# Four product pairs of seven in the down projection of a decoder layer, and the order of the first gate/up pairs

## The chip, the cores and the metric

The kernel runs on one core of a Trainium2 chip. The metric is the device time of one execution in microseconds (us). Before the change three runs took 1966.54, 1968.5 and 1970.39 us: the median is 1968.5.

The engines are called as in the profile: PE is TensorE (PEld its weight load), DVE is VectorE, ACT is ScalarE, POOL is GpSimd, and SP issues the DMAs.

## What is computed

One layer of a decoder with attention, short convolution, a SwiGLU block and a gated embedding, in fp32, for 1024 prompt tokens and 64 sample tokens. The change is in the SwiGLU block:

```
h = rmsnorm(x, norm_ffn)
gu = h @ w_gate_up                      # 1024 x 5632
g, u = gu[..., :D_FF], gu[..., D_FF:]   # D_FF = 2816 = 22 x 128
x = x + (jax.nn.silu(g) * u) @ w_down   # 2816 x 1024
gate = jax.nn.sigmoid(rmsnorm(x, norm_ple) @ w_ple_gate)
return x + (p @ w_ple) * gate
```

## The kernel before

Activations stand transposed, features on the 128 partitions and the 1088 tokens as columns. The second half of the kernel cuts the tokens into two problems, p = 0 and p = 1, of 544 columns, and each into two halves of CW = 272. Every fp32 operand is split into a high and a low part, and a product is three matmuls: high by high, high by low, low by high (`mmg`, L155).

**Gate/up** (`run_pair`, L2372) multiplies by seven products instead of eight. One pair takes column block f of the gate and of the up half, eight row blocks of h as two times four, and one problem p: a 2 by 2 by 2 block product in seven products (`ORDER` 1, 6, 7, 5, 2, 4, 3), each four row blocks x three matmuls = 12 matmuls of 272 columns, 84 in all. Three sides of it cost vector work:

- The activations of a problem need seven factors for each of four row blocks (`factors`, L1819): four half-width tensor operations, the high parts on ACT, and the low parts on DVE, three of 544 columns and one of 272. In the names, `f0` and `f1` are the factors of p = 0 and p = 1. For gate/up they are made out of `norm` (L1930), which writes the normed rows with four operations (L140) per block.
- The weights of a pair arrive as four raw blocks (`wraw`, 256 KB each) and become seven items (`prep`, L520): four sums on DVE (`wsum`), seven high parts on ACT, low parts on DVE for products 6, 5 and 4 and on POOL for 1, 7, 2 and 3 (`wl`, `whl`). There is room for seven items.
- The results of the seven products are added up out of PSUM (`GateUp.take`): product 1 by one ACT operation, the six others by seven DVE operations (product 5 takes two); then silu on ACT and one product on DVE (`q<-q,q`), and a store of the row block of m to `m_scr`. Five PSUM banks (`pj`) take products in turn.

**Down** uses plain products. The 22 row blocks of m form the groups GR = (0,4), (4,6), (10,6), (16,6): first block and number. A group's row blocks are loaded back from `m_scr`, split (`row_in`, `split_row`: high on ACT, low on DVE or POOL in turn) into one of two regions of SBUF, A and B, and multiplied with the eight column blocks k of `w_down` (`down_pass`, `run_rows`). Each product of a group is added to x by one DVE operation (`x<-pj,x`, `evac_down`). Groups 0 and 3 go over four quarters of 272 columns, groups 1 and 2 over three stretches of 384, 384 and 320 (`DOWN_H`). Region A holds the factors of p = 0 until gate/up has ended for p = 0, region B those of p = 1.

**The order** is written by a planner (`Weaver`): PE's work follows the list `order`, and side work (factors, low parts, loads) is put between it by assumed durations. A step of `factors` is let in when DVE's and ACT's assumed backlog behind PE is at most `lag` us, 5.0 for p = 0 and 1.5 for others. Each engine then runs its own list in that order; what the planner assumed plays no part on the chip.

Of the kernel before, what the change touches and what calls it, by code (L numbers as in the profile page):

```python
# [11 lines left out]
F32 = mybir.dt.float32  # L12
# [14 lines left out]
KT = DM // P  # L27
# [289 lines left out]
def hybrid_decoder_step(ctx, tc, I, O):  # L317
# [1612 lines left out]
    def norm(p, gfun, ev):  # L1930
# [6 lines left out]
        W.cur.lag = 5.0 if p == 0 else 1.5  # L1937
# [147 lines left out]
    def down_rows():  # L2085

        for g, (f0, n) in enumerate(GR):
            free = ev_gu[g] if g < 2 else ev_gr[g - 2]
            yield ev_near
            for p in range(2):  # L2090
                left, ahead = [n], []
                for j in range(n):
                    yield ev_ms[f0 + j][p]
                    yield {"Q": 1}
                    q, = getq(1)
                    ahead.append((j, q, W.dma(q, m_scr[f0 + j, :, p * PW:(p + 1) * PW])))
                    if free.t is None and len(ahead) < min(4, n):
                        continue
                    if g not in M:
                        yield free  # L2100
                        r = "AB"[g % 2]
                        M[g] = [Rows(apool if r == "A" else N_["bp"], f"{r}_{e}", f"m{g}_{e}", n) for e in ("hi", "lo")]
                    for j_, q_, t in ahead:
                        W.spawn(row_in(M[g], j_, p, q_, t, left, ev_md[g][p]))
                    ahead.clear()
# [203 lines left out]
    def down_pass(g, ks, ps):  # L2309
        f0, n = GR[g]  # L2310
        bs = [rows_of(I["w_down"], k, lambda *a: evac_down(g, *a), row0=f0 * P, nk=n) for k in ks]
        evs, halves = ev_md[g], None
        if 0 < g < len(GR) - 1:
            ps, halves, evs = tuple(DOWN_H), DOWN_H, dict(zip(DOWN_H, (evs[0], evs[1], evs[1])))
        order.append(("rows", bs, ps, lambda: M[g], evs, 0, ev_gr[g] if ks[-1] == KT - 1 else None, None, halves))
# [13 lines left out]
    for g_ in range(len(GR) - 1):
        down_pass(g_, (0, 1), (0, 1))  # L2330
        for k_ in range(2, KT):
            down_pass(g_, (k_,), (0, 1))
# [172 lines left out]
```

## Time and profile before

| what | before |
|---|---|
| runs, median (lowest to highest) | 1968.5 us (1966.54 to 1970.39) |
| profiled execution, its own time | 1968.76 us |
| its span (first to last instruction) | 1966.6 us |
| PE, DVE, ACT, POOL busy, of the span | 97%, 65%, 36%, 38% |
| granted TensorE clock, mean | 0.989 |

The profiled execution's own time is 2.2 us above its span. A busy PE is not a PE at its peak, since matmuls overlap: a matmul of 272 columns is shown with some 290 ns, while the next begins after about 125 ns. Distances of starts tell the speed.

### The profile page before, as it was taken

How to read it: one execution, taken by the hardware profiler on the slowest of the kernel's cores; microseconds unless marked ns; L12 is line 12 of the kernel's file. 1: busy time of each engine (PE TensorE's matmuls, PEld its weight loads, DVE VectorE, ACT ScalarE, POOL GpSimd, SP SyncE). 2: the span in 40 equal slices, each digit the busy share in tenths (PEclk: the TensorE clock that was granted, in tenths of full speed). 3: DMA queues.
4: the chain of work that ended last, by engine and by line, in shares of the span. 5: the costliest groups of instructions: out<-in, count | busy, mean ns of one | idle time of the engine just before them, and what ended most of it. 6: DMA issues, size and time to landing. Idle time of an engine off the chain costs nothing. (4 is left out here: it accounts for less than half of the span.)

```text
span 1966.6 us, 35775 instructions
## 1 busy us (share of the span) xinstructions
PE 1911.9 (97%) x13337; PEld 1852.8 (94%) x13337; DVE 1269.7 (65%) x2684; ACT 699.3 (36%) x1396; POOL 743.0 (38%) x658
## 2 busy tenths in 40 slices
PE   7999989999999999999999899999999999999998
PEld 5898889998999989989999899999999999999998
DVE  6646999999999975214348875665665643314754
ACT  5355433213443235323335532322322322213543
POOL 2543455223322233114443232332332354424883
PEclk9999999999999999999999999999999999999999
DMA  4565335222322222546443322222222443212343
GB/s 153 167 185 158 98 101 148 53 55 69 85 62 55 63 74 54 153 126 200 134 141 123 133 86 68 79 83 70 78 83 71 133 149 104 91 44 87 106 135 117
DMA packets 291575, 205.21 MB, mean 104 GB/s; under 512 B 28848, under 2 KB 271080, under 8 KB 291402
## 3 DMA queue, kind: packets, MB, share of 16 engines
q1 hardware_dynamic: 291078, 202.58, 34.7%
q8 instruction: 105, 1.72, 0.4%
q14 instruction: 68, 0.56, 0.1%
q10 hardware_dynamic: 324, 0.36, 0.1%
HBM read 151.56 MB, written 51.31 MB: 103 GB/s over the span
## 5 line engine op out<-in xcount | busy, mean ns | idle before, releaser
L151 POOL TENSOR_TENSOR wl<-wraw,wh 128x512 fp32r<-128x512 f32 (+2 forms) x233 | 300.6, 1293 | 680.3 <-ACT wh L132 661.1
L191 PE MATMUL pj<-h_hi,wh 128*128 128x384 f32 (+2 forms) x1197 | 404.4, 338 | 0.3 <-ACT wh L132 0.3
L191 PE MATMUL pj<-h_hi,wl 128*128 128x384 f32 (+2 forms) x1197 | 393.3, 329 | 0.7 <-POOL wl L151 0.7
L191 PE MATMUL pj<-h_lo,wh 128*128 128x384 f32 (+2 forms) x1197 | 393.1, 328 | 0.0
L132 ACT ACTIVATE wh<-wraw 128x512 fp32r<-128x512 f32 (+2 forms) x233 | 141.7, 611 | 299.0 <-PE pj L155 136.1
L191 PEld LDWEIGHTS pj<-h_hi,wh 128*128 128x128 f32 (+1 forms) x1197 | 226.0, 189 | 10.5 <-issue 6.6
L191 PEld LDWEIGHTS pj<-h_lo,wh 128*128 128x128 f32 (+1 forms) x1197 | 226.0, 189 | 2.7
L191 PEld LDWEIGHTS pj<-h_hi,wl 128*128 128x128 f32 (+1 forms) x1197 | 225.3, 188 | 1.7 <-POOL wl L151 1.1
L155 PE MATMUL pj<-f_lo,wh 128*128 128x272 f32 x704 | 203.9, 290 | 6.5 <-DVE f_lo L136 6.5
L155 PE MATMUL pj<-f_hi,wh 128*128 128x272 f32 x704 | 204.2, 290 | 2.0 <-ACT f_hi L132 2.0
L155 PE MATMUL pj<-f_hi,whl 128*128 128x272 f32 x1056 | 206.0, 288 | 0.0
L155 PE MATMUL pj<-f_hi,wl 128*128 128x272 f32 x704 | 204.4, 290 | 0.0
L136 DVE TENSOR_TENSOR x<-pj,x 128x272 f32<-128x272 f32 (+2 forms) x144 | 67.1, 469 | 174.6 <-PE pj L155 171.5
L155 PE MATMUL pj<-m_hi,wh 128*128 128x272 f32 (+2 forms) x586 | 176.1, 300 | 1.0 <-ACT tha L132 0.5
L155 PE MATMUL pj<-m_hi,wl 128*128 128x272 f32 (+2 forms) x586 | 175.7, 300 | 0.0
L155 PE MATMUL pj<-m_lo,wh 128*128 128x272 f32 (+2 forms) x586 | 175.6, 300 | 0.0
L155 PEld LDWEIGHTS pj<-f_hi,whl 128*128 128x128 f32 x1056 | 168.7, 189 | 0.0
L155 PE MATMUL pj<-f_lo,whl 128*128 128x272 f32 x528 | 152.3, 288 | 0.0
L155 PEld LDWEIGHTS pj<-f_lo,wh 128*128 128x128 f32 x704 | 133.6, 190 | 7.2 <-DVE f_lo L136 7.2
L155 PEld LDWEIGHTS pj<-f_hi,wh 128*128 128x128 f32 x704 | 133.6, 190 | 2.4 <-ACT f_hi L132 2.4
L155 PEld LDWEIGHTS pj<-f_hi,wl 128*128 128x128 f32 x704 | 133.9, 190 | 0.2 <-DVE wl L136 0.2
L151 POOL TENSOR_TENSOR whl<-wraw,whl 128x512 fp32r<-128x512 f32 (+1 forms) x67 | 91.3, 1365 | 73.5 <-ACT whl L132 72.9
(371 smaller groups left out, 4474.4 us busy)
## 6 DMA issues: line engine op xcount, KB each, us to landing
wraw<-in_w_in SPq DMA_DIRECT2D x112, 256.0 KB
wraw<-in_w_gate_up SPq DMA_DIRECT2D x92, 256.0 KB
wraw<-in_w_down SPq DMA_DIRECT2D x40, 256.0 KB
wraw<-in_w_out SPq DMA_DIRECT2D x32, 256.0 KB
wraw<-in_w_ple_gate SPq DMA_DIRECT2D x32, 256.0 KB
x<-in_x_prompt SPq DMA_DIRECT2D x13, 512.0 KB
q_hi<-m_scr SPq DMA_DIRECT2D x19, 272.0 KB
m_scr<-q_lo SPq DMA_DIRECT2D x18, 272.0 KB
```

What stands on the lines that cost most here:

```text
L132: self.nc.scalar.activation(out, in_, func, **kw)
L136: self.nc.vector.tensor_tensor(out, a, b, op=op)
L151: self.nc.gpsimd.tensor_tensor(out, a, b, op=op)
L155: self.nc.tensor.matmul(ps, l, r, start=start, stop=stop)
L191: self.nc.tensor.matmul(ps, l, r, start=start, stop=stop)
```

## The change

Of the 22 row blocks of m, blocks 7 to 14 are now multiplied by the seven-product scheme: one pair has the eight row blocks as two times four and the column blocks k and k + 4, so four pairs (k = 0 to 3) for each problem. `DownPair` takes the products as `GateUp` does and then adds the two results to x (two DVE operations of 544 columns, `x<-x,q`). Blocks 0 to 6 and 15 to 21 form two plain groups of seven in quarters of 272 columns. In region order: group 0 in A; the factors of pairs for p = 0 (`fd0`) in B when gate/up has ended; those for p = 1 (`fd1`) in A when group 0 has ended; group 1 in B when the last pair of p = 0 has ended. Some weights are loaded and prepared twice, since only one problem runs with them at a time: k = 0, 1, 2 of group 0 and pairs 0, 1, 2.

In gate/up, pairs f = 0 and 1 run over p = 0 alone, then f = 2 over both, then 0 and 1 over p = 1; before, it was f = 0 over p = 0, f = 1 over both, f = 0 over p = 1. `lag` is 2.5 instead of 1.5 where p isn't 0.

```diff
     def factors(p, b, qa, qb, qt, begun, done):
-        W.cur.lag = 5.0 if p == 0 else 1.5
+        W.cur.lag = 5.0 if p == 0 else 2.5
...
+    class DownPair(GateUp):
+        def finish(self, p, q1, q2):
+            for q, k in ((q1, self.f), (q2, self.f + 4)):
+                yield None
+                xs = N_["x1"][:, k, p * PW:(p + 1) * PW]
+                W.tt(xs, xs, q, OP.add, PW)
+                giveq(q)
...
-    GR = [(0, 4), (4, 6), (10, 6), (16, 6)]
+    GR = [(0, 7), (15, 7)]
+    F_S = 7
+    ev_fd, ev_sx = [Ev(), Ev()], Ev()
...
+        yield ev_near
+        yield from rows_for(0, "A", ev_gu[0])
+        for p, free in ((0, ev_gu[1]), (1, ev_gr[0])):
+            yield free
+            pool, r = (N_["bp"], "B") if p == 0 else (apool, "A")
+            fac["d", p] = [pool.tile([P, 28, CW], F32, tag=f"{r}_{e}", name=f"fd{p}_{e}") for e in ("hi", "lo")]
...
+            for b in range(4):
+                for f in (F_S + b, F_S + 4 + b):
+                    yield ev_ms[f][p]
+                yield {"Q": 3}
+                qs, t = getq(3), 0.0
+                for q, f in zip(qs, (F_S + b, F_S + 4 + b)):
+                    t = W.dma(q, m_scr[f, :, p * PW:(p + 1) * PW])
+                W.spawn(pair_in(p, b, qs, t, done))
+        yield from rows_for(1, "B", ev_sx)
+
+    def pair_in(p, b, qs, t, done):
+        W.cur.t = max(W.cur.t, t)
+        yield None
+        yield from factors(("d", p), b, *qs, Ev(), done)
...
-    for fs_, ps_ in (((0,), (0,)), ((1,), (0, 1)), ((0,), (1,)), (range(2, NF), (0, 1))):
+    for fs_, ps_ in (((0, 1), (0,)), ((2,), (0, 1)), ((0, 1), (1,)), (range(3, NF), (0, 1))):
         gu_pass(fs_, ps_)
...
+    down_pass(0, (0, 1, 2), (0,))
+    down_pass(0, (3, 4, 5, 6, 7), (0, 1))
+    down_pass(0, (0, 1, 2), (1,), ev_gr[0])
+    down_pairs((0, 1, 2), (0,))
+    down_pairs((3,), (0, 1), ev_sx)
+    down_pairs((0, 1, 2), (1,))
     n_before = len(order)
     for p_ in range(2):
-        for k_ in range(KT):
-            down_pass(len(GR) - 1, (k_,), (p_,))
+        down_pass(1, range(KT), (p_,))
```

**DVE at the start of gate/up, before:** the end of the weights of pair 1 and the first evacuations of pair 1 (`q1_lo<-pj`), then the normed rows of block 2 of p = 1 (L140). The low parts of block 1 (`f1_lo`) stand behind all these rows.

```order
L136 TENSOR_TENSOR wl_13035<-wsum_13031,wh_13034 128x512
L136 TENSOR_TENSOR q0_11437<-pj_13102,q0_11437 128x272
L136 TENSOR_TENSOR wl_13067<-wsum_13030,wh_13066 128x512
L136 TENSOR_TENSOR wsum_13122<-wraw_13028,wsum_13031 128x512
L136 TENSOR_TENSOR whl_13100<-wraw_13026,whl_13100 128x512
L136 TENSOR_TENSOR q1_lo_12721<-pj_13143,q1_lo_12721 128x272
L136 TENSOR_TENSOR q1_lo_12721<-pj_13159,q1_lo_12721 128x272
L140 SCALAR_TENSOR_TENSOR q0_hi_11441<-at_12722,gvec_88,x1_11434 128x272
L140 SCALAR_TENSOR_TENSOR q0_hi_11441<-at_12723,gvec_88,x1_11434 128x272
L140 SCALAR_TENSOR_TENSOR q1_11438<-at_12722,gvec_88,x1_11434 128x272
L140 SCALAR_TENSOR_TENSOR q1_11438<-at_12723,gvec_88,x1_11434 128x272
L136 TENSOR_TENSOR q1_lo_12721<-pj_13180,q1_lo_12721 128x272 x2
```

**DVE at the start of gate/up, after:** the same engine around the first evacuations of pair 0 (`q1_lo<-pj`), with the weights of pair 1 behind them.

```order
L136 TENSOR_TENSOR wl_12976<-wsum_12794,wh_12975 128x512
L136 TENSOR_TENSOR wsum_12996<-wraw_12931,wsum_12795 128x512
L136 TENSOR_TENSOR q1_lo_12721<-pj_13013,q1_lo_12721 128x272
L136 TENSOR_TENSOR whl_12993<-wraw_12639,whl_12993 128x512
L136 TENSOR_TENSOR f1_lo_12719<-q1_11438,f1_hi_12718 128x544
L136 TENSOR_TENSOR f1_lo_12719<-q0_lo_11442,f1_hi_12718 128x544
L136 TENSOR_TENSOR wsum_13042<-wraw_12981,wraw_13038 128x512
L136 TENSOR_TENSOR wsum_13043<-wsum_13042,wraw_12933 128x512
L136 TENSOR_TENSOR q1_lo_12721<-pj_13031,q1_lo_12721 128x272
```

Two low parts of block 1 now stand a pair earlier, among the evacuations of pair 0 and ahead of the sums and low parts of pair 1's weights.

**DVE in the middle of the down projection, before:** group 2's evacuations, three of each column block, with nothing else between them.

```order
L136 TENSOR_TENSOR x1_11434<-pj_19268,x1_11434 128x384
L136 TENSOR_TENSOR x1_11434<-pj_19292,x1_11434 128x384
L136 TENSOR_TENSOR x1_11434<-pj_19312,x1_11434 128x320
L136 TENSOR_TENSOR x1_11434<-pj_19340,x1_11434 128x384
L136 TENSOR_TENSOR x1_11434<-pj_19364,x1_11434 128x384
```

**DVE in the same part, after:** from the evacuation of product 6 of the first down pair on (`q0_hi<-pj`), with the sums of the next pair's weights (`wsum`), the half-width operations for the factors of p = 1 (`q1_hi<-`) and the low part of the next pair's product 6 (`wl`).

```order
L136 TENSOR_TENSOR q0_hi_11441<-pj_19512,q0_hi_11441 128x272
L136 TENSOR_TENSOR wsum_19530<-wraw_19363,wraw_19467 128x512
L136 TENSOR_TENSOR wsum_19531<-wsum_19530,wraw_19361 128x512
L136 TENSOR_TENSOR q0_lo_11442<-pj_19537,q0_hi_11441 128x272
L136 TENSOR_TENSOR wsum_19551<-wraw_19361,wraw_19363 128x512
L136 TENSOR_TENSOR q1_hi_12720<-q1_hi_12720 128x272
L136 TENSOR_TENSOR q1_hi_12720<-q0_hi_11441,q1_hi_12720 128x272 x2
L136 TENSOR_TENSOR q0_lo_11442<-pj_19556,q0_lo_11442 128x272
L136 TENSOR_TENSOR q0_hi_11441<-pj_19556,q0_hi_11441 128x272
L136 TENSOR_TENSOR q0_hi_11441<-pj_19579,q0_hi_11441 128x272
L136 TENSOR_TENSOR wl_19535<-wsum_19531,wh_19534 128x512
```

What had been one evacuation for each product is now, between two evacuations, a weight's sum or low part or a factor's operation, and PE's product 6 of the next pair waits for the last row shown.

## Rows read from the trace of the kernel before

**Rows 1.** The page, busy time of the engines (part 1), and the span in 40 equal slices of 49 us (part 2): the line of DVE, each digit the busy share of a slice in tenths.
```profile
PE 1911.9 (97%) x13337; PEld 1852.8 (94%) x13337; DVE 1269.7 (65%) x2684; ACT 699.3 (36%) x1396; POOL 743.0 (38%) x658
...
DVE  6646999999999975214348875665665643314754
```

**Rows 2.** The chain of work that ended last, its longest piece (start us, us, what).
```profile
1588.05 221.07 PE pj L155 x1488
```

**Rows 3.** Timeline of PE (start us, us, engine, line, operation, out<-in, shape) where the parts of the down projection begin and end: the first matmul of group 0, the first of groups 1 and 2 (384 columns), the second of group 3, the first after the projection (h_hi).
```profile
1575.37 0.29 PE L155 MATMUL pj<-m_hi,wh 128*128 128x272 f32 x1
...
1624.31 0.34 PE L155 MATMUL pj<-m_hi,wh 128*128 128x384 f32 x1
...
1766.80 0.29 PE L155 MATMUL pj<-m_lo,whl 128*128 128x272 f32 x1
...
1840.99 0.28 PE L155 MATMUL pj<-h_hi,wh 128*128 128x272 f32 x1
```

**Rows 4.** Busy time in stretches (us from the span's start; length; busy us and number of operations of PE, weight load, DVE, ACT, POOL; granted clock; DMA share; GB/s): the start of gate/up, its steady part, groups 1 and 2 of the down projection.
```profile
1109.40:1120.00 10.60, 10.59 (x84) 10.37 (x84) 10.03 (x20) 4.46 (x8) 4.29 (x3) 1.00 0.39 117
1120.00:1131.60 11.60, 3.08 (x16) 2.01 (x14) 11.46 (x26) 5.36 (x10) 0.00 (x0) 0.74 0.09 33
...
1150.00:1550.00 400.00, 400.00 (x3187) 400.00 (x3186) 252.39 (x439) 115.93 (x210) 114.55 (x76) 1.00 0.25 78
...
1625.00:1766.00 141.00, 141.00 (x857) 141.00 (x857) 42.58 (x59) 29.29 (x56) 53.46 (x43) 1.00 0.25 76
```

**Rows 5.** Timeline of PE at the start of gate/up: the matmuls before which it waited (in brackets: the wait and what ended it), and two that follow.
```profile
1122.67 0.39 PE L155 MATMUL pj<-f_lo,wh 128*128 128x272 f32 x1 [1.67 <-DVE f_lo L136]
...
1127.67 0.60 PE L155 MATMUL pj<-f_lo,wh 128*128 128x272 f32 x1 [4.36 <-DVE f_lo L136]
...
1130.52 0.59 PE L155 MATMUL pj<-f_hi,wh 128*128 128x272 f32 x1 [2.03 <-ACT f_hi L132]
...
1131.58 0.60 PE L155 MATMUL pj<-f_lo,wh 128*128 128x272 f32 x1 [0.46 <-DVE f_lo L136]
...
1132.43 0.43 PE L155 MATMUL pj<-f_lo,wh 128*128 128x272 f32 x1
1132.65 0.43 PE L155 MATMUL pj<-f_hi,wl 128*128 128x272 f32 x1
```

**Rows 6.** Timeline of DVE from the first factor of the second half of the columns (1084.48) to the last (1132.08), rows with each kind of operation.
```profile
1084.48 0.97 DVE L140 SCALAR_TENSOR_TENSOR q<-at,gvec,x 128x272 f32<-128x272 f32 x2 [3.40 <-PE at L187]
...
1096.96 0.44 DVE L136 TENSOR_TENSOR f_lo<-q_hi,f_hi 128x272 fp32r<-128x272 f32 x1 [1.60 <-ACT f_hi L132]
1100.33 0.69 DVE L136 TENSOR_TENSOR wl<-wsum,wh 128x512 fp32r<-128x512 f32 x1 [2.93 <-ACT wh L132]
...
1104.09 1.25 DVE L136 TENSOR_TENSOR whl<-wraw,whl 128x512 fp32r<-128x512 f32 x1
...
1108.02 0.69 DVE L136 TENSOR_TENSOR wsum<-wraw 128x512 f32<-128x512 f32 x1
1108.62 0.43 DVE L136 TENSOR_TENSOR q_hi<-pj,q_hi 128x272 f32<-128x272 f32 x1
1108.97 0.78 DVE L136 TENSOR_TENSOR q<-pj,q 128x272 f32<-128x272 f32 x2
...
1115.60 0.90 DVE L140 SCALAR_TENSOR_TENSOR q_hi<-at,gvec,x 128x272 f32<-128x272 f32 x2
1116.41 0.90 DVE L140 SCALAR_TENSOR_TENSOR q<-at,gvec,x 128x272 f32<-128x272 f32 x2
...
1119.66 0.44 DVE L136 TENSOR_TENSOR q_lo<-q_lo,q_hi 128x272 f32<-128x272 f32 x1
...
1126.89 1.35 DVE L136 TENSOR_TENSOR f_lo<-q_hi,f_hi 128x544 fp32r<-128x544 f32 x2
...
1132.08 0.43 DVE L136 TENSOR_TENSOR f_lo<-q,f_hi 128x272 fp32r<-128x272 f32 x1
```

**Rows 7.** Timeline of POOL (GpSimd) beside it: two low parts of weights.
```profile
1103.49 1.30 POOL L151 TENSOR_TENSOR whl<-wsum,whl 128x512 fp32r<-128x512 f32 x1 [1.29 <-ACT whl L132]
1104.74 1.74 POOL L151 TENSOR_TENSOR wl<-wraw,wh 128x512 fp32r<-128x512 f32 x1
```

**Rows 8.** DVE by shape in the steady part of gate/up, 1150 to 1550 us, 19 pairs (count | busy us, mean ns | idle before): five of the seven operations on a pair's weights.
```profile
L136 DVE TENSOR_TENSOR wl<-wsum,wh 128x512 fp32r<-128x512 f32 x38 | 36.4, 959 | 0.0
L136 DVE TENSOR_TENSOR wsum<-wraw 128x512 f32<-128x512 f32 x39 | 30.6, 784 | 0.0
L136 DVE TENSOR_TENSOR whl<-wraw,whl 128x512 fp32r<-128x512 f32 x19 | 20.4, 1071 | 5.2 <-ACT whl L132 5.2
```

**Rows 9.** POOL by shape in the same stretch, one of four groups.
```profile
L151 POOL TENSOR_TENSOR whl<-wsum,whl 128x512 fp32r<-128x512 f32 x19 | 24.6, 1295 | 43.7 <-ACT whl L132 43.7
```

**Rows 10.** Timeline of POOL and of DVE in group 0, three and two low parts of a row block of m side by side.
```profile
1583.32 5.45 POOL L151 TENSOR_TENSOR m_lo<-q_hi,m_hi 128x544 fp32r<-128x544 f32 x3
...
1584.21 3.33 DVE L136 TENSOR_TENSOR m_lo<-q_lo,m_hi 128x544 fp32r<-128x544 f32 x2
```

**Rows 11.** Other places where PE waited and the granted clock after them: a wait in the attention part, the stretch around it, and the stretch after the waits of rows 5.
```profile
837.66 0.30 PE L198 MATMUL pt<-ident,kraw 128*128 128x128 f32 x1 [2.46 <-DMA kraw<-in_cache_k]
...
834.00:843.00 9.00, 5.76 (x33) 4.40 (x33) 3.46 (x6) 3.23 (x6) 3.58 (x4) 0.81 0.47 135
...
1132.00:1135.80 3.80, 3.80 (x18) 3.80 (x18) 1.08 (x4) 0.92 (x2) 1.28 (x1) 0.50 0.00 0
```

More of the change, by code (lines that the diff above doesn't have):

```diff
@@ L1936, in norm @@
             room(p)
-        W.cur.lag = 5.0 if p == 0 else 1.5
+        W.cur.lag = 5.0 if p == 0 else 2.5
         yield {"at": 2, "Q": 1}
@@ L2085, in down_rows @@
     def down_rows():
[L2087 to L2105, printed above, removed]
+        yield ev_near
@@ new lines, in down_rows, with done @@
+        yield from rows_for(0, "A", ev_gu[0])
[3 more added lines that the diff above has]
+            fac["d", p] = [pool.tile([P, 28, CW], F32, tag=f"{r}_{e}", name=f"fd{p}_{e}") for e in ("hi", "lo")]
+            left = [4]
+            def done(p=p, left=left):
+                left[0] -= 1
+                if left[0] == 0:
+                    ev_fd[p].t = W.cur.t
+            for b in range(4):
[6 more added lines that the diff above has]
+                W.spawn(pair_in(p, b, qs, t, done))
@@ new lines, in down_rows, with rows_for @@
+        yield from rows_for(1, "B", ev_sx)
[3 more added lines that the diff above has]
+        yield from factors(("d", p), b, *qs, Ev(), done)
+    def rows_for(g, r, free):
+        f0, n = GR[g]
+        for p in range(2):
+            left, ahead = [n], []
+            for j in range(n):
+                yield ev_ms[f0 + j][p]
+                yield {"Q": 1}
+                q, = getq(1)
+                ahead.append((j, q, W.dma(q, m_scr[f0 + j, :, p * PW:(p + 1) * PW])))
+                if free.t is None and len(ahead) < min(4, n):
+                    continue
+                if g not in M:
+                    yield free
+                    M[g] = [Rows(apool if r == "A" else N_["bp"], f"{r}_{e}", f"m{g}_{e}", n) for e in ("hi", "lo")]
+                for j_, q_, t in ahead:
+                    W.spawn(row_in(M[g], j_, p, q_, t, left, ev_md[g][p]))
+                ahead.clear()
@@ L2118, in evac_down @@
     def evac_down(g, k, p, h, ps):
-        c0, n = DOWN_H[p][h] if p in DOWN_H else (p * PW + h * CW, CW)
+        c0, n = p * PW + h * CW, CW
         xs = N_["x1"][:, k, c0:c0 + n]
@@ L2124, in evac_down @@
             W.spawn(add_square(p, k, n_down, g_ple, ev_h3, how=norm_rows))
-    DOWN_H = {f"c{c}": {c // 2: CH[c]} for c in range(3)}
     PLE_H = {0: {0: (0, CW), 1: (CW, CW)}, 1: {"a": SEG["a"], "b": SEG["b"]}}
@@ L2307, in gu_pass, with down_pass, down_pairs @@
                 order.append(("pair", x, p, p == ps[-1], ev_gu[p] if f == NF - 1 else None))
-    def down_pass(g, ks, ps):
+    def down_pass(g, ks, ps, ev_done=None):
         f0, n = GR[g]
[L2311 to L2315, printed above, removed]
+        for k in ks:
+            bs = [rows_of(I["w_down"], k, lambda *a: evac_down(g, *a), row0=f0 * P, nk=n)]
+            order.append(("rows", bs, ps, lambda: M[g], ev_md[g], 0, ev_done if k == ks[-1] else None))
+    def down_pairs(ks, ps, ev_done=None):
+        for k in ks:
+            x = pair_of(I["w_down"], F_S * P, 4, k * P, (k + 4) * P), DownPair(k)
+            for p in ps:
+                order.append(("pair", x, p, p == ps[-1], ev_done if p == 0 else None, True))
     def ple_pass(p):
@@ L2325, in hybrid_decoder_step @@
     n_gu = len(order)
-    for fs_, ps_ in (((0,), (0,)), ((1,), (0, 1)), ((0,), (1,)), (range(2, NF), (0, 1))):
+    for fs_, ps_ in (((0, 1), (0,)), ((2,), (0, 1)), ((0, 1), (1,)), (range(3, NF), (0, 1))):
         gu_pass(fs_, ps_)
     n_near = len(order) - 2
[L2329 to L2332, printed above, removed]
+    down_pass(0, (0, 1, 2), (0,))
[4 more added lines that the diff above has]
+    down_pairs((0, 1, 2), (1,))
     n_before = len(order)
     for p_ in range(2):
-        for k_ in range(KT):
-            down_pass(len(GR) - 1, (k_,), (p_,))
+        down_pass(1, range(KT), (p_,))
     for p_ in range(2):
@@ L2370, in run_rows, with run_pair @@
                     yield None
-    def run_pair(x, p, last, ev_done):
+    def run_pair(x, p, last, ev_done, down=False):
         items, sink = x
-        yield ev_h2[p]
+        yield (ev_fd if down else ev_h2)[p]
         blocks = range(4)
@@ L2386, in run_pair @@
             for kk, b in enumerate(blocks):
-                th, tl = factor(p, i, b)
+                th, tl = factor(("d", p) if down else p, i, b)
                 for w_, a_ in ((it["hi"], th), (it["hi"], tl), (it["lo"], th)):
```

## The prediction

> **What bounds the kernel now.** I read the page first, then the chain of waits, then the timelines of PE and of DVE where the change lies. PE is busy for 97% of the span, and DVE is near full in some slices alone [rows 1]. The chain ends in PE: its longest piece is 221 us of one line of matmuls [rows 2]. So time goes down by fewer or shorter matmuls, or by taking away waits of PE, and it goes up wherever another engine falls behind PE. Of the waits, those that matter lie at the start of gate/up, where PE waits four times, 8.5 us in all, for factors of the second problem [rows 5].
>
> **The matmuls of the down projection.** In the steady part of gate/up 3187 matmuls of 272 columns start in 400 us, 0.1255 us each [rows 4]. Group 0 (384 matmuls) takes from 1575.37 to 1624.31, 48.9 us; groups 1 and 2 (864) to 1766.7, 142.4 us; group 3 (576) to 1840.99, 74.3 us [rows 3]. The last holds some 1.9 us of the norm's small matmuls, which stay. Before: 265.6 us. After: two groups of seven have 2 x 7 x 8 x 4 x 3 = 1344 matmuls, eight pairs 8 x 84 = 672, all of 272 columns: 2016 x 0.1255 = 253.0 us, and 1.9 us for the norm. **-10.7 us** if nothing else waits. There are 192 more matmuls, but 574,464 columns become 548,352: wide matmuls turn into narrow ones, so the gain is below the eighth that the scheme saves on its part.
>
> **The start of gate/up.** The order before puts DVE's low parts of block 1 behind the weights of pair 1; after, they stand a pair earlier, and a third pair over p = 0 runs ahead of the first need. I sum DVE from the first normed row of p = 1 (1084.48) to the last low part. Distances of starts are 0.35 us for an evacuation (0.78 for two, less one of 0.43), 0.41 for a normed row, 0.60 for a weight's operation, 0.36 for half-width, 0.63 for a low part of 544 [rows 6]. Before there are 16 normed rows, 20 half-width operations, 14 of 544, 14 on weights, 14 evacuations: 6.6 + 7.2 + 8.8 + 8.4 + 4.9 = 35.9 us. It took 48.0 us, 1084.48 to 1132.5 [rows 6]; 4.5 us of the rest are two waits, and 7 us are smaller gaps and operations lengthened beside POOL. After, 7 more on weights and 7 more evacuations (counted in the order) stand ahead of the last one: 42.6 us. To this I add 0.5 us for each of 12 POOL operations (worked out below), 1.6 us for the wait at 1096.96, which nothing moves, and 2 us of small gaps: 52 us, so the last factor is there at about 1137, and PE ends the first product of p = 1 at about 1137.5 instead of 1132. By then it has done 84 matmuls more, 10.5 us of work: 5.0 us gained. Before, the granted clock was 0.50 from 1132 to 1135.8, with starts 0.22 us apart instead of 0.125 [rows 5, 11]: 17 matmuls, 1.7 us, which I count as gained too, since I expect three waits of 1 to 2.5 us in place of one of 4.4. Together **-6.7 us**. Bounds: -12 if DVE hides all, -1 if the third pair's own work delays the factors by as much as it covers. Pairs over one problem, each with weights of its own, go on behind it: weights 4.6 + 2 x 0.69 (rows 8, below), evacuations 7 x 0.35, the silu's product 0.63 to 1.4, some 9.5 us of DVE for every 10.5 of PE; **+0.5 us**.
>
> **The price on DVE in the pair stage.** This isn't in the trace of before in this place: groups 1 and 2 leave DVE at 42.6 of 141 us [rows 4]. The nearest rows are those of gate/up. Eight pairs over a problem have: 8 x 7 evacuations on DVE x 0.35 = 19.6 us; 16 adds to x of 544, 10.1 us; weights for seven pairs, the first mostly ahead of the stage, 6 x 7 x 0.60 = 25.2; the factors of p = 1, which can't begin before group 0 has left region A, 4 blocks x (4 x 0.36 + 3 x 0.63 + 0.36) = 14.8; the low parts of group 1, eight on DVE, 5.0; some 2 us at the seam. That is 76.7 us of DVE, beside 84.3 us of PE. Alone it would fit. But an operation between two SBUF operands is lengthened when POOL runs: 0.69 us alone, 1.25 beside POOL at 1104.09 [rows 6, 7]. In gate/up five of the seven weight operations of a pair take (36.4 + 30.6 + 20.4)/19 = 4.6 us instead of 5 x 0.69 = 3.4 [rows 8], and the silu products bear some more: I take 2 us for four POOL operations, 0.5 each. The stage has some 34 of them (six pairs' weights and the end of the first's, 28; six low parts of group 1): 17 us. DVE needs 94 us for 84.3. Most of it falls early: the order puts 36.6 us of DVE's rows (at the same distances) between the end of group 0 and the low part for product 6 of pair 3, with 11 or 12 POOL operations, 6 us, while PE has 3 x 10.5 + 1.8 = 33.4 us. So I take **+10.5 us**: PE waits for the low part of product 6 of pairs 1, 2 and 3 (`wl`), and once for a PSUM bank. Bounds: +3 (DVE's own work alone, early part) and +16 (next).
>
> A low part on POOL takes 1.29 us alone and 1.74 beside DVE [rows 7, 9], and three of 544 on POOL with two on DVE fill 5.45 us [rows 10]: they take turns. The Trainium skill (SBUF — State Buffer, section "Who interferes with whom") has it as an exclusive lock: a DVE operation with two SBUF inputs and a GpSimd operation that reads SBUF keep each other out for whole instructions. The rows agree; taken strictly, all 34 POOL operations and DVE's two-SBUF operations would stand in one line, and the stage would come out as in rival 2.
>
> **Edits with little price.** Group 0 now needs seven low rows of p = 0 by 1575, where four of p = 0 sufficed. They have the last pair's 10.5 us, and with turns three on POOL and four on DVE take 3 x 1.82 + 4 x 0.63 = 8.0 us [rows 6, 10]: 0, and 3 if late. The adds to x, stores and the tail (p = 0's norm under p = 1's matmuls, now 42 instead of 36 us) cost nothing on PE. More weight loads (pairs: 1 MB per 10.5 us, 100 GB/s; gate/up's start ran at 117 [rows 4]) are hidden by that.
>
> **Sum.** 1968.8 (the profiled execution, 0.3 above the median of the runs) - 10.7 - 6.7 + 0.5 + 10.5 = 1962.4; I add 1 us for the seams: **1963.4 us**. Own range 1959 to 1968.
>
> **Rivals.**
> 1. *DVE keeps up.* The low parts of weights are ready in time, since five banks and seven weight places let PE run 4 products ahead: the stage costs 2 instead of 10.5 us, 1955. For it: gate/up, with pairs of the same kind over two problems, has no wait after 1136. Against: there DVE is busy 252 of 400 us [rows 4] with the weights spread over twice the matmuls.
> 2. *The strict turn.* 34 x 1.29 = 44 us of POOL and 55 us of DVE's two-SBUF work (25.2 + 10.1 + 14.8 + 5.0) in 84.3 us: +15, 1968. Against it: in rows 10 a turn of both takes 1.82 us, less than 1.36 + 0.63.
> 3. *The clock falls* (the other side). PE's waits of 2.5 us and more are followed by half clock: a wait of 2.46 us at 837.66 by a stretch with 0.81, rows 5's waits by 0.50 [rows 11]. If five waits in the pair stage are each followed by 5 us of half clock, PE loses 5 x (1 - 0.1255/0.22) = 2.1 us each, 11 in all; what falls within DVE's backlog is hidden, and it decides once the slow stretches outlast it: 1974. Against it: most of the waits that I expect are shorter than 2.46 us, the shortest here with a low clock behind it.
> 4. *The factors of p = 1 come no earlier*: the third pair brings 14 DVE operations of its own, so the first term is near 0: 1970.
>
> **How the numbers follow.** Chances: forecast 0.50, rival 1 0.20, rival 2 0.12, rival 3 0.11, rival 4 0.07. The range takes in rival 1 with some more and rival 3: 1953 to 1974. Within 0.2% of 1968.5 (about what a measurement of this kernel can tell from no change) is 1964.6 to 1972.4. Of the forecast's own range 1959 to 1968 some three fifths lie below: 0.50 x 0.62 + 0.20 = 0.51 faster; slower are four fifths of rival 3 and a fifth to a third of rivals 2 and 4: 0.13; same 0.36.
>
> **What would show it.** Right: the down projection takes about 265 us again, with matmuls 0.1255 us apart and waits, ended by DVE `wl`, before product 6 of the second to fourth pair; DVE above 90% there; at the start of gate/up waits below 3 us each, the first product of p = 1 ended by 1138, granted clock 1.00. Wrong: a down projection below 258 us (rival 1), a clock of 0.5 in the pair stage (rival 3), a wait over 4 us at the first product of p = 1 (rival 4), or waits at the start of group 0, which I price at nothing.

## The result and the profile after

The changed kernel takes 1979.69 us (median of five runs, 1975.72 to 1982.54) against 1968.5: ratio 1.0056, 95% interval 1.0044 to 1.0069. It is slower by some 11 us, outside the predicted range of 1953 to 1974. The profiled execution, the slowest of the five, took 1982.54 us; its span is 1980.7.

The page after, busy time of the engines and the slices of DVE, against [rows 1]:

```profile
PE 1911.2 (96%) x13529; PEld 1849.1 (93%) x13529; DVE 1363.8 (69%) x2822; ACT 731.6 (37%) x1458; POOL 769.2 (39%) x662
...
DVE  6546999999999965214348986666666765984654
```

PE has 192 matmuls more and is busy for 0.7 us less. DVE has 138 operations and 94 us more, and its slices 35 and 36 (1684 to 1783 us) now read 9 and 8 where [rows 1] has 3 and 1.

The borders of the stages are read off the timeline of PE (first matmul with a factor `f`, with `m`, with `fd`, with `m` again, with `h`). Busy time in these four stretches of the changed kernel (us from the span's start; length; busy us and number of operations; granted clock; DMA share; GB/s):

```profile
core 0: us, PE busy (x) PEld busy (x) DVE busy (x) ACT busy (x) POOL busy (x), PEclk, DMA share, GB/s
1100.71:1574.26 473.55, 467.74 (x3699) 466.74 (x3698) 320.89 (x541) 152.67 (x278) 151.25 (x100) 0.99 0.28 88
1574.26:1662.12 87.86, 84.92 (x674) 84.48 (x673) 45.60 (x78) 24.59 (x44) 34.77 (x26) 1.00 0.38 118
1662.12:1770.38 108.26, 92.77 (x674) 90.64 (x673) 103.48 (x154) 44.44 (x85) 54.84 (x34) 0.92 0.35 104
1770.38:1856.94 86.56, 86.56 (x689) 86.38 (x687) 45.75 (x83) 33.09 (x57) 51.89 (x42) 1.00 0.35 102
```

| stage, us | before [rows 3] | predicted | after |
|---|---|---|---|
| to the first matmul of gate/up | 1098.95 | 1098.95 | 1100.71 |
| gate/up | 476.4 | 470.2 | 473.6 |
| down: group 0 | 48.9 | 84.3 | 87.9 |
| down: groups 1, 2; now pairs | 142.4 | 94.8 | 108.3 |
| down: last group | 74.3 | 86.2 | 86.6 |
| rest (norm, gate of the embedding, end) | 125.6 | 125.6 | 123.8 |

The down projection takes 282.7 us instead of 265.6. The loss is in the pair stage: PE needs 84.3 us there, the stage takes 108.3, and DVE is busy for 103.5 of them. The longer of PE's waits (timeline, in brackets the wait and what ended it; the first row is from the start of gate/up, two from group 0, five from the pair stage):

```profile
1130.05 0.59 PE L155 MATMUL pj<-f_hi,wl 128*128 128x272 f32 x1 [4.34 <-DVE wl L136]
...
1597.01 0.39 PE L155 MATMUL pj<-m_hi,whl 128*128 128x272 f32 x1 [1.36 <-DVE x L136]
...
1601.51 0.40 PE L155 MATMUL pj<-m_hi,whl 128*128 128x272 f32 x1 [1.57 <-DVE x L136]
...
1674.71 0.59 PE L155 MATMUL pj<-fd_hi,wh 128*128 128x272 f32 x1 [3.39 <-DVE q_hi L136]
...
1687.40 0.40 PE L155 MATMUL pj<-fd_hi,whl 128*128 128x272 f32 x1 [1.50 <-ACT q_lo L132]
...
1693.03 0.36 PE L155 MATMUL pj<-fd_hi,wh 128*128 128x272 f32 x1 [0.85 <-ACT wh L132]
...
1698.40 0.59 PE L155 MATMUL pj<-fd_hi,wl 128*128 128x272 f32 x1 [4.88 <-DVE wl L136]
...
1743.72 0.82 PE L155 MATMUL pj<-fd_hi,whl 128*128 128x272 f32 x2 [2.10 <-DVE whl L136]
```

The chain of waits, which in [rows 2] ran through PE alone from 1588 to 1809, now leaves PE at 1671.33 and goes mostly through DVE's operations (from 1683 to 1687 through ACT's) until PE has it again at 1710.93, and once more from 1720 to 1743.72 (three of its pieces: start us, us, what):

```profile
1671.33 2.97 DVE fd_lo L136 x5
...
1710.93 9.05 PE pj L155 x70
...
1743.72 31.37 PE pj L155 x226
```

Three waits are followed by a lower granted clock (windows, columns as above): 0.50, the 1.2 GHz level.

```profile
1674.70:1678.10 3.40, 3.39 (x15) 3.40 (x16) 3.33 (x8) 1.71 (x4) 0.37 (x1) 0.50 0.56 185
...
1698.40:1702.00 3.60, 3.60 (x16) 3.60 (x17) 3.60 (x8) 1.06 (x3) 0.35 (x1) 0.50 0.21 62
1743.70:1749.70 6.00, 5.98 (x26) 5.98 (x27) 5.86 (x11) 1.01 (x2) 1.10 (x1) 0.50 0.29 87
```

What lengthens DVE is seen where its timeline and that of POOL lie side by side. DVE in the pair stage, four operations with two inputs from SBUF and two evacuations (`<-pj`):

```profile
1674.22 0.43 DVE L136 TENSOR_TENSOR q_hi<-pj,q_hi 128x272 f32<-128x272 f32 x1
...
1683.97 1.81 DVE L136 TENSOR_TENSOR x<-x,q_lo 128x544 f32<-128x544 f32 x1
...
1693.43 1.79 DVE L136 TENSOR_TENSOR fd_lo<-q_lo,fd_hi 128x544 fp32r<-128x544 f32 x1
1695.14 1.78 DVE L136 TENSOR_TENSOR fd_lo<-q_hi,fd_hi 128x544 fp32r<-128x544 f32 x1
...
1702.39 0.72 DVE L136 TENSOR_TENSOR x<-x,q_lo 128x544 f32<-128x544 f32 x1
...
1735.44 0.43 DVE L136 TENSOR_TENSOR q<-pj,q 128x272 f32<-128x272 f32 x1
```

POOL at the same times:

```profile
1683.86 1.34 POOL L151 TENSOR_TENSOR wl<-wsum,wh 128x512 fp32r<-128x512 f32 x1 [2.91 <-ACT wh L132]
...
1692.99 1.65 POOL L151 TENSOR_TENSOR wl<-wsum,wh 128x512 fp32r<-128x512 f32 x1 [3.38 <-ACT wh L132]
1694.60 1.74 POOL L151 TENSOR_TENSOR whl<-wraw,whl 128x512 fp32r<-128x512 f32 x1
...
1734.89 1.76 POOL L151 TENSOR_TENSOR whl<-wraw,whl 128x512 fp32r<-128x512 f32 x1
```

POOL's first operation ends at 1685.20 and DVE's add to x at 1685.78, 0.58 us later; the next two end at 1694.64 and 1696.34, DVE's low parts at 1695.22 and 1696.92, again 0.58 later. So DVE starts when POOL has ended. The evacuation at 1735.44, with one input from SBUF and one from PSUM, lies wholly inside a POOL operation and takes 0.43 as ever. DVE's first evacuation of a pair's product comes at 1674.22, behind the factor work of two blocks: until then the products fill the five PSUM banks, which is the wait of 3.39 us. Up to 1716 us the stage has lost 15 us against PE's pace of 0.1255 us a matmul, and 9 us more behind it, where 21 of the 34 POOL operations begin.

### The profile page after: what moved, and what is told of

Its sections match the earlier page's. It is cut to its first block, busy times and chain, and to the rows that moved or that the text cites. A ratio compares the mean times of both kernels' runs of the same rounds, so it can differ in the third digit from the quotient of the medians.

```text
span 1980.7 us, 36447 instructions
## 1 busy us (share of the span) xinstructions
PE 1911.2 (96%) x13529; PEld 1849.1 (93%) x13529; DVE 1363.8 (69%) x2822; ACT 731.6 (37%) x1458; POOL 769.2 (39%) x662
## 4 chain that ended last, share of the span: by engine, by line
PE 74%; DVE 15%; issue 4%; DMA 3%; POOL 2%; ACT 1%; SPq 1%; DVEq 0%; POOLq 0%; ACTq 0%
PE pj L155 39%; PE pj L191 24%; PE at L187 4%; DVE junk L1235 4%; PE po L187 3%; PE pt L198 3%; DVE ru L136 1%; SPq L164 1%; DVE fd_lo L136 1%; POOL wl L151 1%; DVE q_lo L136 1%; DVE cv L140 1%; DVE wsum L136 1%; DMA qh<-qh_scr 1%; DVE cum L1271 1%
## 5 line engine op out<-in xcount | busy, mean ns | idle before, releaser
L151 POOL TENSOR_TENSOR wl<-wraw,wh 128x512 fp32r<-128x512 f32 (+2 forms) x231 | 307.8, 1335 | 633.1 <-ACT wh L132 621.8
L191 PEld LDWEIGHTS pj<-h_hi,wh 128*128 128x128 f32 (+1 forms) x1197 | 226.2, 189 | 11.6 <-issue 7.0
L155 PE MATMUL pj<-m_hi,wh 128*128 128x272 f32 x490 | 141.9, 290 | 0.5 <-ACT tha L132 0.5
L155 PE MATMUL pj<-m_hi,wl 128*128 128x272 f32 x490 | 141.5, 289 | 0.0
L155 PE MATMUL pj<-m_lo,wh 128*128 128x272 f32 x490 | 141.4, 289 | 0.0
L151 POOL TENSOR_TENSOR whl<-wraw,whl 128x512 fp32r<-128x512 f32 (+1 forms) x67 | 102.2, 1529 | 45.0 <-ACT whl L132 44.9
L151 POOL TENSOR_TENSOR wl<-wsum,wh 128x512 fp32r<-128x512 f32 x38 | 63.3, 1667 | 129.9 <-ACT wh L132 129.9
```

The costliest lines, as they stand in the source:

```text
L151: self.nc.gpsimd.tensor_tensor(out, a, b, op=op)
L155: self.nc.tensor.matmul(ps, l, r, start=start, stop=stop)
L191: self.nc.tensor.matmul(ps, l, r, start=start, stop=stop)
```

## The experiments

Theory 1: in the pair stage the amount of DVE work sets the time, and each POOL operation beside it adds 0.8 us to that work, since the two take turns. Theory 2: the loss is in the order (a burst of factor work ahead of the first evacuations) and in the half clock behind the waits; DVE's total would do. For gate/up the question is what of the two edits (third pair, lag) brings how much. The kernel before took 1967.7 to 1968.2 us (medians) on the chips of these runs.

**The two halves apart.** e1 takes the gate/up half into the kernel before, e3 the down half (the changed kernel with the old first pairs and lag 1.5 for p = 1 in gate/up; the down pairs keep 2.5). The lag stands in two places, in `factors` and in `norm`, and both are changed.

```diff
# e1, in the kernel before; e3 makes the opposite edit in the changed kernel
-    for fs_, ps_ in (((0,), (0,)), ((1,), (0, 1)), ((0,), (1,)), (range(2, NF), (0, 1))):
+    for fs_, ps_ in (((0, 1), (0,)), ((2,), (0, 1)), ((0, 1), (1,)), (range(3, NF), (0, 1))):
...
-        W.cur.lag = 5.0 if p == 0 else 1.5
+        W.cur.lag = 5.0 if p == 0 else 2.5
```

> The kernel before with the gate/up half of the change alone: pairs 0 and 1 over p = 0, 2 over both, 0 and 1 over p = 1, and lag 2.5; the down projection is left as before. The prediction's term was -6.2 us (-6.7 for the start, +0.5 for the single pairs): 1962.3. The trace of the changed kernel shows gate/up 476.4 us long before and 473.6 after, with a wait of 4.3 us and half clock still in it: by that only -2.9, 1965.6. If the order of the first pairs is worth nothing and the 2.9 us are scatter: 1968.5.

> The changed kernel with gate/up as before (pair 0 over p = 0, 1 over both, 0 over p = 1, lag 1.5 for p = 1 there): the down half of the change alone. If the two halves add up, as the stages of the trace say (gate/up -2.9, down projection +17.1, tail -1.9): 1979.7 + 2.9 = 1982.6. By the prediction's sizes the down half would be +0.8 (1969.3). If the two halves disturb one another (a late end of gate/up that delays the rows of group 0), it is nearer to 1975, and the waits of 1.4 and 1.6 us in group 0 are gone.

e1: 1963.71 us, ratio 0.9978 (0.9970 to 0.9987), gate/up 473.0 us. e3: 1984.2 us, ratio 1.0078 (1.0065 to 1.0091), its pair stage 108.25 us and group 0 with the two waits again (1.18 and 1.57 us). The halves add up: 0.9978 x 1.0078 is 1.0056. The down half by itself loses 15 to 16 us.

**POOL out of the pair stage, two ways.** In e4 DVE makes all low parts of a down pair's weights; in e5 the four of POOL are left out and ACT writes the weight itself in their place. The flag `down`, set where a down pair's weights are made, keeps gate/up as it is.

```diff
# e4
-                (W.tt if kind in (6, 5, 4) else W.pool_tt)(flat(l), ...)
+                (W.tt if kind in (6, 5, 4) or kind and it["pair"]["down"] else W.pool_tt)(flat(l), ...)
# e5
+                if kind in (1, 7, 2, 3) and it["pair"]["down"]:
+                    W.act(flat(l), src, AF.Copy, n)
+                else:
...
```

> The changed kernel with all seven low parts of a down pair's weights on DVE, none on POOL. Theory 1, DVE and POOL take turns: in the pair stage 34 POOL operations lengthened DVE's by 27.7 us, 0.81 each, while a low part costs DVE 0.60 between starts. 28 move: 75.8 us of DVE alone + 28 x 0.60 + 6 x 0.81 + 5 us idle = 102.5 us for the stage instead of 108.3, 1974. Theory 2, a POOL operation costs DVE 0.5 as in gate/up and the rest of the loss is the half clock and the order of DVE's work at the seam: DVE gets 28 x 0.1 = 3 us more, 1982.

> The changed kernel in which four of the seven low parts of a down pair's weights (those that POOL makes) are left out: ACT copies the weight in their place, so that the same tiles are written and the same matmuls run. POOL has only six low parts of group 1 in the pair stage. Theory 1 (turns of DVE and POOL are the loss): DVE has 75.8 + 6 x 0.81 + up to 5 idle = 81 to 86 us for PE's 84.3, the stage falls from 108.3 to some 87, 1958. Theory 2 (burst of factor work ahead of the first evacuation, half clock behind each wait): the wait of 3.4 us at the first PSUM bank, the half clock behind it and most of the others stay, at least 8 us: the stage is 97 or more, 1968.

e4: 1979.04 us, 1.0055 (1.0042 to 1.0069), no better than the changed kernel. e5: 1969.1 us, 1.0005 (0.9996 to 1.0013). Their pair stages, e4 first (columns as above):

```profile
1657.90:1767.95 110.05, 93.74 (x675) 90.76 (x673) 99.65 (x179) 44.88 (x86) 15.40 (x10) 0.94 0.36 106
```

```profile
1658.00:1756.41 98.41, 89.12 (x675) 86.53 (x673) 84.14 (x154) 58.22 (x112) 15.32 (x11) 0.98 0.40 120
```

e5 has the same 154 DVE operations as the changed kernel and 23 POOL operations less, and DVE is busy for 84.1 instead of 103.5 us: 0.84 us for each POOL operation. That is the price here, a mean without a model. But the stage fell to 98.4 only, where theory 2 had it, with DVE idle for 14 us: something besides the turns is in it. e4 fits neither time. DVE's busy time did fall by 3.8 us (25 operations of 0.6 added, 24 POOL operations of 0.84 gone: -5), but new idle time took it back. The waits of DVE in e4's stage (us in total, times, longest):

```profile
DVE wsum L136 <- DMA wraw<-in_w_down: 6.2, 3, 2.9
```

By the code a place for raw weights is free only when its low parts are made; made later on DVE, they would let the next load start later. That this is the cause of the waits is read from the code, not tested.

In the steady part of gate/up of the kernel before, the price can be read too. The silu's products stand there in groups beside POOL's operations and in groups apart from them (two of the groups, columns as in [rows 8]):

```profile
L136 DVE TENSOR_TENSOR q_lo<-q_lo,q_hi 128x544 f32<-128x544 f32 x12 | 16.5, 1374 | 15.7 <-ACT q_lo L132 15.7
...
L136 DVE TENSOR_TENSOR q_hi<-q_hi,q_lo 128x544 f32<-128x544 f32 x11 | 8.0, 725 | 8.0 <-ACT q_hi L132 8.0
```

19 of them take 1.37 instead of 0.73 us, 12 us in all, and the groups of [rows 8] some 21 us more than at 0.69 each: 33 us for 76 POOL operations [rows 4], 0.44 each.

**The order of the factor work.** e8 holds the down pairs' factors back with a lag of 0.5; e10 does the same in e5.

```diff
-        W.cur.lag = 5.0 if p == 0 else 2.5
+        W.cur.lag = 5.0 if p == 0 else 2.5 if p == 1 else 0.5
```

> The changed kernel with lag 0.5 instead of 2.5 for the factors of the down pairs alone: the factor work of p = 1 stands further behind the evacuations of the first pairs, nothing is left out. Theory 1 (DVE is short of time through the stage): only the place of the waits moves, 1978 to 1981. Theory 2 (the burst of factor work ahead of the first evacuation makes the first wait of 3.4 us, its half clock and a backlog): without it 6 us less, 1974.

> The lows-on-ACT kernel (four of the seven low parts of a down pair's weights left out, ACT copies in their place, no POOL beside the pairs) with lag 0.5 for the down pairs' factors. If turns with POOL and the burst of factor work at the seam are separate losses that add up, the stage falls from 98.4 by the 3 to 6 us that lag 0.5 brought with POOL: 93 to 95 and 1964 to 1966. If without POOL DVE has time enough and the burst is hidden by itself, nothing changes: 1969.

e8: 1974.0 us, 1.0030 (1.0019 to 1.0041), the time that theory 2 gave, but, as the stages show, not for its reason alone. e10: 1958.59 us, 0.9956 (0.9942 to 0.9969), less than either expected. Group 0 and the pair stage of e8:

```profile
1572.79:1657.91 85.12, 84.96 (x675) 84.61 (x673) 45.47 (x78) 24.33 (x44) 34.49 (x26) 1.00 0.39 121
```

```profile
1657.91:1763.20 105.29, 90.08 (x674) 85.61 (x673) 103.81 (x154) 44.73 (x85) 52.76 (x34) 1.00 0.36 108
```

and the pair stage of e10:

```profile
1656.44:1746.63 90.19, 86.50 (x675) 84.79 (x673) 83.03 (x154) 58.40 (x112) 15.03 (x11) 1.00 0.44 133
```

In e8, 2.7 us of the gain are group 0's two waits and only 3.0 the pair stage, half of theory 2's 6. There is no half clock left in the stage (1.00), and it still takes 105.3 us: DVE is busy for 103.8 of them. So with POOL this order and the half clock are worth 3 us, and DVE's amount of work the other 21. Without POOL the same edit is worth 8.2 us (98.4 to 90.2): DVE then has time to spare (busy for 84 of 98 us), and its order was in the way. The two causes don't add: each hides part of the other. e8 and e10 give the price of a POOL operation once more, with 154 DVE operations in both: (103.8 - 83.0)/23 = 0.90 us, where DVE is busy for 99% of e8's stage.

**The factors of p = 1 left out.** In e6 ACT copies rows of m into the 28 places; e7 does this in e5. e11 is e6 with block b made after pair b - 1 of p = 0; e12 has that gate alone (`ev_pk[k]` comes when pair k of p = 0 has ended).

```diff
# e6, e7, e11: in factors()
+        if p == ("d", 1):
+            for q, s, n in ((qb, 2, 2), (qa, 0, 2), (qa, 4, 2), (b21, 6, 1)):
+                lead(q, s, n)
+                W.act(part(lo, s, n).bitcast(F32R), q, AF.Copy, n * CW)
...
# e11, e12: in down_rows()
+                if p == 1 and b > 0:
+                    yield ev_pk[b - 1]
...
```

> The changed kernel in which the differences and low parts of the down pairs' factors of p = 1 are left out: ACT copies rows of m into the 28 places, DVE does nothing for them. POOL's low parts stay. In the lows-on-ACT run, with no POOL beside the pairs, the stage still took 98.4 us with DVE 84 us busy. Theory 1, DVE's own work in the first part of the stage is the second half of the loss: 14.8 us less of DVE, 61 + 27.6 of lengthening = 89 and 4 idle: the stage 93, 1965. Theory 2, the turns of DVE and POOL and the chain of a pair's weights (sum on DVE, high part on ACT, low part on DVE) make the loss and the factors only fill gaps: 101 or more, 1973.

> Both leavings at once: POOL's low parts of the down pairs' weights replaced by ACT copies, and the differences and low parts of the factors of p = 1 replaced by ACT copies. DVE has 61 us plus some 5 of lengthening. If turns and factor work are the whole loss, the pair stage runs at PE's 84.3 to 87 us, 1957. If the chain of a pair's weights over a single problem is too long by itself, 92 or more, 1963.

e6: 1975.91 us, 1.0039 (1.0026 to 1.0053). e7: 1972.62, 1.0022 (1.0013 to 1.0031), slower than e5, which does more. Both fell to a wait that the edit itself brought (waits of PE in e6's pair stage):

```profile
PE pj L155 <- ACT q L132: 9.8, 1, 9.8
```

ACT's copies of all four blocks stood ahead of its evacuation of the first product; e7 has the same wait (10.4 us). The stage times of these two runs tell nothing of the theories; e11 mends it. But their stages, e6 first, have the same 122 DVE operations:

```profile
1655.79:1760.94 105.15, 90.68 (x674) 89.57 (x673) 85.53 (x122) 52.03 (x101) 54.92 (x34) 0.92 0.35 107
```

```profile
1661.02:1762.61 101.59, 88.37 (x675) 87.06 (x673) 69.88 (x122) 66.50 (x128) 15.26 (x11) 0.93 0.38 116
```

A POOL operation costs DVE 15.65/23 = 0.68 us here, where DVE is busy for 81% of the stage and idle for 16 us in a single wait.

> The kernel without differences and low parts of the factors of p = 1 (ACT copies in their place, POOL as in the changed kernel), now with block b of these factors loaded and copied only after pair b - 1 of p = 0, so that ACT's copies don't stand ahead of the first evacuation (there ACT kept PE waiting for 9.8 us). Theory 1, DVE's amount of work is the bound in the first four pairs: DVE has 52 - 15 = 37 us there for 42 us of PE, so no wait over 1 us is left in that half; the second half, untouched, keeps its 5.3 us of waits: the stage is 93, 1965. Theory 2, the weights' chain and the turns are the bound: 100 or more, 1972.

> The changed kernel with block b of the factors of p = 1 made only after pair b - 1 of p = 0, nothing left out: the 14.8 us of factor work spread over the four pairs of p = 0. Theory 1 (amount of work): DVE still needs some 52 us for that half, 10 more than PE, so the stage stays at 102 to 106, 1974 to 1977, as with lag 0.5. Theory 2 (burst): below 100, 1970.

e11: 1964.25 us, 0.9979 (0.9970 to 0.9988). e12: 1980.17 us, 1.0063 (1.0049 to 1.0077). e11, the first pairs and the whole stage:

```profile
1657.09:1708.00 50.91, 50.91 (x407) 50.88 (x406) 42.93 (x67) 32.95 (x65) 24.86 (x16) 1.00 0.55 171
1657.09:1751.08 93.99, 88.83 (x675) 87.74 (x674) 83.94 (x122) 52.04 (x101) 54.37 (x35) 0.96 0.44 135
```

e12, the stage, and two of PE's waits in it:

```profile
1659.86:1768.72 108.86, 92.26 (x674) 89.99 (x673) 102.69 (x154) 45.23 (x85) 50.28 (x34) 0.91 0.38 116
```

```profile
1718.10 0.59 PE L155 MATMUL pj<-fd_hi,wh 128*128 128x272 f32 x1 [4.55 <-ACT fd_hi L132]
...
1723.61 0.60 PE L155 MATMUL pj<-fd_lo,wh 128*128 128x272 f32 x1 [4.92 <-DVE fd_lo L136]
```

With POOL at work as in the changed kernel, but without DVE's part of these factors, PE has no wait for the first 51 us, and the stage takes 94.0 us, as theory 1 had it (93). So the chain of a pair's weights (theory 2 of e6 and e11) holds PE up nowhere in the first four pairs. With the same gate and the work left in, it takes 108.9, more than either theory said and as much as without the gate: of PE's 16.5 us of waits 11 now stand at the first product of p = 1, which lacks its factors. The work can be moved, and in these two runs its amount came out elsewhere.

**The start of gate/up.** All have the old down projection. e2 has three first pairs with lag 1.5, e9 the old pairs with lag 2.5, e13 the old pairs with lag 5.0, e14 three first pairs with lag 5.0.

```diff
# e9, in the kernel before (e13: 5.0 in place of 2.5)
-        W.cur.lag = 5.0 if p == 0 else 1.5
+        W.cur.lag = 5.0 if p == 0 else 2.5
```

> The gate/up half alone with lag 1.5 instead of 2.5 (three pairs over p = 0 first, the rest as in the kernel before). With lag 2.5 it measured 1963.7 and still has one wait of 4.3 us, for the low part of product 6 of pair 2, on DVE behind the differences of block 2 of the factors of p = 1. If that insertion is the cause of the wait, the smaller lag puts weights ahead of it: the wait shrinks to 1 or 2 us and its half clock goes, 1960. If DVE simply has too much to do before the first product of p = 1, the wait moves to the factors and the time stays at 1963 to 1965.

> The kernel before with lag 2.5 instead of 1.5 for p = 1 and nothing else: gate/up in the old order of pairs, the old down projection. Lag 2.5 with three first pairs measured 1963.7, lag 1.5 with three first pairs 1968.6, the same as before. If the lag alone brings the gain: 1964. If the gain needs both (a third pair that covers DVE, and factor work let in ahead of the weights): 1967 to 1970.

> The kernel before with lag 5.0 instead of 1.5 for p = 1, old order of pairs and old down projection: the factors of p = 1 go still further ahead of weights. Lag 2.5 measured 1963.3, with waits of 1.2, 0.8 and 3.4 us left (the last two for factors) and DVE idle for 2.7 us after the last factor. If the order decides: the wait for factors shrinks by another 2 to 3 us, 1960. If the amount of DVE work decides: the waits change from factors to weights and the time stays at 1962 to 1965.

> The gate/up half alone (three first pairs over p = 0) with lag 5.0. With lag 2.5 it measured 1963.7 with one wait of 4.35 us for weights of pair 2 that stand behind factor work. If the order decides, more factor work ahead of weights makes that wait longer: 1966 or more. If the amount of DVE work decides: 1963 to 1965.

| lag for p = 1 | old pairs | three first pairs |
|---|---|---|
| 1.5 | 1967.7 to 1968.5 (before) | 1968.6, 1.0003 (0.9994 to 1.0012) |
| 2.5 | 1963.27, 0.9981 (0.9972 to 0.9990) | 1963.71, 0.9978 (0.9970 to 0.9987) |
| 5.0 | **1960.63, 0.9963 (0.9951 to 0.9976)** | 1966.2, 0.9996 (0.9986 to 1.0005) |

The third pair brings nothing at 1.5 and 2.5 and costs 5.6 us at 5.0 (e2 came out above both of its expectations). The lag brings all of the gain, and it is the order that decides (e13, e14 as expected by it), not the mere amount of DVE's work. In e2 the waits at weights and at factors stand together, the longest at the first product of p = 1 (two of three):

```profile
1124.29 0.54 PE L155 MATMUL pj<-f_hi,wl 128*128 128x272 f32 x1 [3.14 <-DVE wl L136]
...
1139.90 0.60 PE L155 MATMUL pj<-f_lo,wh 128*128 128x272 f32 x1 [4.16 <-DVE f_lo L136]
```

PE's waits of 0.8 us and more from 1107 to 1145 in e9:

```profile
1111.67 0.40 PE L155 MATMUL pj<-f_hi,wl 128*128 128x272 f32 x1 [1.15 <-DVE wl L136]
1122.40 0.40 PE L155 MATMUL pj<-f_lo,wh 128*128 128x272 f32 x1 [0.82 <-DVE f_lo L136]
1126.46 0.59 PE L155 MATMUL pj<-f_lo,wh 128*128 128x272 f32 x1 [3.42 <-DVE f_lo L136]
```

All of PE's waits from 1105 to 1145 in e13:

```profile
1108.74 0.52 PE L155 MATMUL pj<-f_hi,whl 128*128 128x272 f32 x2 [2.63 <-DVE whl L136]
1115.28 0.40 PE L155 MATMUL pj<-f_hi,wl 128*128 128x272 f32 x1 [0.22 <-DVE wl L136]
```

And the last one in e14:

```profile
1128.63 0.40 PE L155 MATMUL pj<-f_hi,wl 128*128 128x272 f32 x1 [2.78 <-DVE wl L136]
```

In e13 the factors of p = 1 are in time, and gate/up takes 470.0 us (1097.58 to 1567.59) instead of 476.4. A third pair has 14 DVE operations and four on POOL of its own for the 10.5 us that it covers, and its weights are what PE then waits for. e13 beats both the kernel before and the changed one.

## Why the prediction was wrong, point by point

- **Columns, -10.7 us: right.** The last group took 86.6 us (predicted 84.3 + 1.9), and group 0 without its waits of 1.36 and 1.57 us takes 84.9.
- **Start of gate/up, -6.7 + 0.5: half of it to some two thirds, and for another reason.** The trace gives -2.9, e1 against before some -4.4. A smaller step failed here: that the third pair, which moves the need for factors 10.5 us back at the price of 14 DVE operations, gains by it. With lag 1.5 it gains nothing (e2), and a wait of 4.16 us stands at the first product of p = 1: that is rival 4, with the sign that was named for it. With lag 2.5 the wait moves from the factors to the third pair's own weights (4.34 us before `wl` in place of the waits of [rows 5]). What gained is the lag, which I priced only as a part of the new order.
- **Pair stage, +10.5: 24.0. This is the step that failed.** The mechanism was right, DVE short of time beside POOL. DVE's own work was sized rightly: e5's 84.1 us less 11 x 0.84 is 74.9, against 76.7 with 2 for the seam in it. What was off is "0.5 each" for a POOL operation, taken from gate/up [rows 8]: in this stage it is 0.84, and 34 x 0.34 = 11.6 of the missing 13.5 us. For gate/up itself 0.5 was right (0.44). In gate/up DVE is busy for 252 of 400 us [rows 4], so part of POOL's operations fall where DVE has nothing to do; in the pair stage DVE nearly always has the next operation ready. The prices bear this out in the main: 0.44, 0.68, 0.84 and 0.90 us with DVE busy for 63%, 81%, 96% and 99%. But e11 against e7, which differ in the gate too, gives 0.59 at 89%, so the busy share alone doesn't set the price; whether the share of operations with two inputs from SBUF counts too was not tried. The rows of a dense stretch were there: in [rows 10] two low parts beside three of POOL take 3.33 us instead of 2 x 0.63, 1.0 us more for each. I judged them as rival 2 and took the mean of an airy stretch for the sum. The other 2 us are DVE's idle time, 4.8 us in the stage where the sum left some 3; e8 has 1.5. Of the waits that I named, the one for a PSUM bank came (3.39 us) and one of the three for `wl` (4.88 us, third pair); the rest ended mostly on ACT or on `whl`.
- **Rival 2, the strict turn: right in its mechanism, short in its sum.** The ends 0.58 us apart show that whole operations keep each other out, and evacuations run beside POOL. Its +15 (99 us for PE's 84.3) left out the evacuations that fall where POOL stands idle, some 4.5 us if DVE's 103.5 us are set against it, and DVE's 4.8 us of idle time. The Trainium skill (SBUF — State Buffer, section "Who interferes with whom") says that a DVE instruction with at most one SBUF input, outside the two-port modes, doesn't contend with GpSimd, and one with two does with a GpSimd instruction that reads SBUF. The trace agrees on both, with 0.43 us beside POOL for the one and 1.8 instead of 0.7 for the other.
- **Rival 3, the clock: there, and small.** Three stretches at 0.50 follow waits of 3.39, 4.88 and 2.10 us. Without them (e8) the stage is 3.0 us shorter, and that includes the better order. That DVE's backlog hides the rest, the rival's own condition, fits DVE's 103.5 busy us of 108.3, but no run shows it apart.
- **Edits at no price.** Group 0's start cost 3.5 us. The prediction named 3, if the low rows were late; they were not. The two waits are for PSUM banks, whose evacuations (`x<-pj`) stand on DVE behind the factors of p = 0 (at 1591.73, 1596.52 and 1601.03, with factor work between); with the factors held back (e8) group 0 takes 85.1 us. The rest after the projection is 1.9 us shorter, and the part ahead of gate/up was 1.8 us longer in this execution (in e13's it ends at 1097.58); neither was followed further.

Open is how much of the idle time of the changed kernel's pair stage is the seam and how much the clock; they were not parted.

## What to carry to other kernels

Price interference by a stretch as dense as the one that will be, not by a mean over a stretch with slack: a POOL operation that costs DVE 0.44 us where DVE is two thirds busy costs 0.84 where it is nearly full. Before a scheme trades matmuls for vector work, sum the vector engine's time for the stage with that price; when it comes to PE's time or more, little is gained by moving work within the stage (3 us of 24 in e8, nothing in e12). And part an edit of two pieces before crediting one: here one constant gave all of a gain that the reordering beside it was meant to give, and raising it further, without the reordering, gave more (e13).

## What was not expected of the hardware

- One POOL operation that reads SBUF costs a full DVE 0.84 us, more than the 0.60 us for which DVE does the same low part itself. Handing work to POOL there loses DVE's time, and taking it back (e4) gained nothing either: DVE was busy for 3.8 us less and waited longer, for loads among others.
- Waits alike in length are not followed by the same clock. In the changed kernel the wait of 2.10 us at 1743.72, shorter than the 2.46 us that rival 3 took for the shortest, has 0.50 behind it. e8 has the same wait for the same `whl` at the same place of the program (1736.56), and the clock stays at 1.00 (the matmul, and the stretch behind it):

```profile
1736.56 0.52 PE L155 MATMUL pj<-fd_hi,whl 128*128 128x272 f32 x2 [2.10 <-DVE whl L136]
```

```profile
1736.60:1740.00 3.40, 3.40 (x27) 3.40 (x28) 3.30 (x6) 0.00 (x0) 1.04 (x1) 1.00 0.52 154
```

What differs between the two wasn't tried; in e13 a wait of 2.63 us has means of 0.70 and 0.66 in the two stretches behind it. So a price for the clock can't be read off the length of a wait alone.
